# The last three modulation chunks of layer 0: one load step at a time in place of two

## The chip, the cores and the metric

The kernel runs on one core of one Trainium2 chip. The metric is device time in microseconds (us) of one execution; lower is better.

## The reference

The program is a two-layer trunk over 256 latent and 256 context tokens of width 2048. Layer 0 mixes tokens by centred pooling, layer 1 by neighbourhood attention; each is followed by a gated MLP of width 5504. Before every sub-layer, a normalised stream is scaled and shifted, and its result is gated, by vectors that are computed from a conditioning vector:

```python
silu_c, silu_cc = jax.nn.silu(c), jax.nn.silu(c_ctx)
for i in range(DEPTH):
    ml = (silu_c @ w_mod[i] + b_mod[i]).reshape(B, 6, 1, D)
    mc = (silu_cc @ w_mod[i] + b_mod[i]).reshape(6, 1, 1, D)
    a_lat = modulate(rms_norm(h, norm1_g[i]), ml[:, 0], ml[:, 1])
    ...
    h = h + ml[:, 2] * y_lat
    h = h + ml[:, 5] * conv_ffn(modulate(rms_norm(h, norm2_g[i]), ml[:, 3], ml[:, 4]), ...)
```

The change concerns `silu_c @ w_mod[0]` and `silu_cc @ w_mod[0]`, the modulation of layer 0: a matrix of 2048 x 12288 float32 (about 100 MB) is read once, for two vectors.

## The kernel before

**Chunks and steps.** The 12288 columns of layer 0's modulation are 24 chunks of 512. `mod_pe` works through one chunk in four steps. A step loads 2 tiles of 128 x 1024 float32 (512 KB each, line 131, tile `wm`), and multiplies them with the two vectors on TensorE in four products (line 207, tile `mod`), each in a 32-column strip of the array of its own (`tile_position`), so that the four run beside one another. The products of all four steps add up in one PSUM bank with the tag `m`, of which there is one. After the fourth step ScalarE copies the bank out (line 219, `modev`); at the start of the next chunk TensorE turns the copy by four transposes (line 224, `modt`), and VectorE sums and finishes it (line 226 and `finish_mod`).

**Pairs of steps.** In the kernel before, the first step of a pair (g = 0 or 2) only loads. The second one (g = 1 or 3) loads and then issues eight products in a row, its own four first, then those of the step held back. The first of the eight waits for all four loads of the pair; the others are tied behind it, so that nothing comes between them.

**Buffers.** `stage` hands out weight buffers in turn from the list `rooms`: six of its own and those lent from the activation tiles by `lend`. All weights pass through the same list. In the stretch that matters here the lent buffers have been taken back (`LENT`, at half 13 of group 3), so six buffers remain, three pairs: two 512 KB tiles for each step of modulation and two for each load of other weights. A load into a buffer waits, on the load queue (SP), until the buffer's last reader is done.

**What runs beside it.** `partial(g, ...)` computes the first eight blocks of layer 0's gate and up projections for input group g, with weights `wcg` (gate) and `wcu` (up), four blocks at a time; each load is split into a high part by a cast on ScalarE (line 147) and a low part by a subtraction on VectorE (line 149), and 48 matmuls follow (lines 566 to 568, `cg` and `cu`), beside a shift term (lines 549 and 582, `pwg`, `pwu`, `ptg`, `ptu`). Between them, at 32 places ("halves") for each g, `between` calls `need`, which pumps the generator of modulation steps to a count that grows by 20 in 32 halves. In group 3 the steps pumped are 79 to 96, of which 81 to 84 are chunk 20, 85 to 88 chunk 21, 89 to 92 chunk 22 and 93 to 96 chunk 23. Then the rest of layer 0's MLP follows, its first matmuls in line 653.

**Order.** The Python order gives priorities; the scheduler then sets each engine's instruction order at build time by its own estimate of when each instruction is ready. `tc.high_priority()` and `tc.issue_after(...)` adjust that. On the chip every queue runs in that order.

Of the kernel before, what the change touches and what calls it, by code (L numbers as in the profile page):

```python
# [59 lines left out]
def kernel(ctx: ExitStack, tc: tile.TileContext, xT, cxT, wmod, wg, wu, wd, wp,  # L60
# [10 lines left out]
    def bank(tag, name):  # L71

        if tag == "d" and nbank[0] is not None:
            nbank[0] += 1
            if nbank[0] % 4 == 0:
                tag = "m"
        return pp.tile([P, 512], F32, tag=tag, bufs={"gu": 4, "d": 3, "m": 1}[tag], name=name)
# [45 lines left out]
    fetched = []  # L123

    def load(src, cols, name):

        ts = []
        for j in range(0, cols, 1024):
            n = min(1024, cols - j)
            t = stage(f"{name}_{j}")  # L130
            fetched.append(nc.sync.dma_start(t[:, :n], src(j, j + n)).ins)
            ts.append((t, n))
        return ts
# [27 lines left out]
    def mod_tile(l, ch):  # L161

        return main.tile([P, 4, 2], F32, tag=f"modT{ch if ch < 20 else (l, ch)}", name=f"modT{l}_{ch}")

    def by_row(ps):

        return ps.rearrange("p (i j c) -> p i c j", i=4, j=4)[:, :, 0:2, :]
# [9 lines left out]
    def finish_mod(l, ch, streams, src):  # L177

        mt = src[0] if len(src) == 1 else mod_tile(l, ch)
        n = len(streams)  # L180
        which, q = divmod(ch, 4)

        def dup(name, a):
            return V(name)[:, a : a + 8].rearrange("p (i s) -> p i s", s=2)[:, :, 0:n]

        bias = dup(f"bm_{l}", 8 * ch)
        for b, v in enumerate(src):
            own = slice(32 * b, 32 * b + 32) if len(src) > 1 else slice(0, P)
            nc.vector.tensor_tensor(mt[own, :, 0:n], v, bias[own], op=ALU.add)
        if which in (1, 4):  # L190
            nc.vector.scalar_tensor_tensor(mt[:, :, 0:n], mt[:, :, 0:n], 1.0, dup(f"g{1 if which == 1 else 2}_{l}", 8 * q),
                                           op0=ALU.add, op1=ALU.mult)
        modT[l, ch] = mt

    def mod_pe(l, ch, sc, pool):

        ps = bank("m", f"mod{l}_{ch}")
        for g in range(4):
            ts = load(lambda a, b: wmod[l, ch, g, :, a:b], 2048, f"wm{l}_{ch}_{g}")
            if g % 2 == 0:  # L200
                held, first = ts, fetched[-2:]
            else:
                landing = first + fetched[-2:]
                with ExitStack() as behind:
                    for n, (gg, tt) in enumerate(((g, ts), (g - 1, held))):
                        for j in (2, 3, 0, 1):
                            ins = nc.tensor.matmul(ps[32 * j : 32 * j + 32, :], sc[:, 4 * gg + j, :],  # L207
                                                   tt[j // 2][0][:, 512 * (j % 2) : 512 * (j % 2) + 512],
                                                   start=(g == 1 and n == 0), stop=(g == 3 and n == 1),
                                                   tile_position=(0, 32 * j))  # L210
                            if n == 0 and j == 2:
                                for x in landing:
                                    tc.add_manual_dep(ins.ins, x.name, mybir.DependencyInfo(
                                        mybir.DependencyClass.Sync, mybir.DependencyReason.DATA), reason="whole")
                                behind.enter_context(tc.issue_after(ins.ins))
                                behind.enter_context(tc.high_priority())
            if g == 3:
                ev = pool.tile([P, 512], F32, tag="t2", name=f"modev{l}_{ch}")
                nc.scalar.copy(ev, ps)
            yield  # L220
        with tc.high_priority():
            p2 = bank("d", f"modt{l}_{ch}")
            for i in range(4):
                nc.tensor.transpose(p2[:, P * i : P * i + P], ev[:, P * i : P * i + P], ident)
        r = mod_tile(l, ch)
        nc.vector.tensor_reduce(out=r, in_=by_row(p2), axis=AX.X, op=ALU.add)
        finish_mod(l, ch, both, [r])
# [116 lines left out]
    with ExitStack() as ph0:  # L344
# [62 lines left out]
        with ExitStack() as phs:  # L407
# [32 lines left out]
            def mods():  # L440

                for g in range(4):
                    for w in (0, 1, 2, 4):
                        yield from mod_pe(0, 4 * w + g, sc, f0)
                    yield from mod_pe(0, 12 + g, sc, f0)
                    shifts(g)
                for q in range(4):
                    yield from mod_pe(0, 20 + q, sc, f0)
# [805 lines left out]
```

## Time and profile before

| | |
|---|---|
| median of 3 runs | 3062.89 us (3062.56 to 3066.64) |
| the profiled execution | 3060.9 us |
| its span, first to last instruction | 3059.1 us |
| mean granted TensorE clock | 0.989 |
| TensorE (PE) busy | 2977.4 us, 97% |
| VectorE (DVE) busy | 1939.4 us, 63% |
| ScalarE (ACT) busy | 1371.3 us, 45% |
| read from memory | 554.93 MB, 182 GB/s over the span |

Times in the profile are counted from the first instruction. PE is the matmul part of TensorE, PEld its weight loads, SPq the queue that issues the loads. In a row of the timeline, the first number is the start, the second the length, and `x16` a count of instructions (a product with float32 operands is two); a bracket tells how long the engine had been idle before it and what ended that. A granted clock of 1.00 is full speed.

### The profile page before, as it was taken

How to read it: one execution, taken by the hardware profiler on the slowest of the kernel's cores; microseconds unless marked ns; L12 is line 12 of the kernel's file. 1: busy time of each engine (PE TensorE's matmuls, PEld its weight loads, DVE VectorE, ACT ScalarE, POOL GpSimd, SP SyncE). 2: the span in 40 equal slices, each digit the busy share in tenths (PEclk: the TensorE clock that was granted, in tenths of full speed). 3: DMA queues.
4: the chain of work that ended last, by engine and by line, in shares of the span. 5: the costliest groups of instructions: out<-in, count | busy, mean ns of one | idle time of the engine just before them, and what ended most of it. 6: DMA issues, size and time to landing. Idle time of an engine off the chain costs nothing.

```text
span 3059.1 us, 40876 instructions
## 1 busy us (share of the span) xinstructions
PE 2977.4 (97%) x15082; PEld 2416.9 (79%) x15082; DVE 1939.4 (63%) x2748; ACT 1371.3 (45%) x2219; POOL 829.1 (27%) x823
## 2 busy tenths in 40 slices
PE   5999989999999999999999999999999999999998
PEld 2666668888888888888887888878888888888887
DVE  4455764386584857758586656474767666666666
ACT  3433455323333242433334444343545666666665
POOL 2111313303122030321312000000003566566665
PEclk9999989999999999999999999999999999999999
DMA  9888563384765747567482333333355555555563
GB/s 390 331 305 321 207 206 97 103 255 142 216 192 166 241 143 234 160 198 212 150 257 69 121 101 114 101 107 111 106 161 182 185 181 196 192 187 182 184 196 113
DMA packets 177927, 559.70 MB, mean 183 GB/s; under 512 B 17600, under 2 KB 22208, under 8 KB 177728
## 3 DMA queue, kind: packets, MB, share of 16 engines
q1 hardware_dynamic: 177728, 557.10, 55.7%
q8 instruction: 119, 1.95, 0.2%
q14 instruction: 80, 0.66, 0.1%
HBM read 554.93 MB, written 2.10 MB: 182 GB/s over the span
## 4 chain that ended last, share of the span: by engine, by line
PE 93%; DMA 2%; DVE 1%; POOL 1%; ACT 1%; issue 1%; SPq 0%; DVEq 0%; ACTq 0%; POOLq 0%
PE g L788 5%; PE u L788 5%; PE d L679 5%; PE d L680 5%; PE d L681 5%; PE d L835 4%; PE g L653 4%; PE g L655 4%; PE g L654 4%; PE u L655 4%; PE u L653 4%; PE u L654 4%; PE g L791 3%; PE u L791 3%; PE mod L207 2%; PE d L839 2%
## 5 line engine op out<-in xcount | busy, mean ns | idle before, releaser
L692 POOL TENSOR_TENSOR hl<-hl,dy 128x256 f32<-128x256 f32 x160 | 146.2, 914 | 941.8 <-ACT dy L691 941.6
L850 POOL TENSOR_TENSOR hl<-hl,dy 128x256 f32<-128x256 f32 x320 | 332.1, 1074 | 188.3 <-ACT dy L848 186.0
L262 DVE SCALAR_TENSOR_TENSOR macc<-wm,sc,macc 128x512 f32<-128x512 f32 (+1 forms) x360 | 328.8, 944 | 66.9 <-DMA wm<-wmod 66.2
L691 ACT ACTIVATE dy<-d,modT 128x256 f32<-128x256 f32 x320 | 133.1, 469 | 187.5 <-PE d L681 167.2
L692 POOL TENSOR_TENSOR hc<-hc,dy 128x256 f32<-128x256 f32 x160 | 129.4, 809 | 0.0
L848 ACT ACTIVATE dy<-d,modT 128x512 f32<-128x512 f32 x160 | 104.5, 684 | 43.0 <-PE d L839 41.5
L149 DVE TENSOR_TENSOR wd_2l<-wd,wd_2h 128x1024 fp32r<-128x1024 f32 (+1 forms) x44 | 54.5, 1245 | 107.8 <-ACT wd_2h L147 106.6
L207 PE MATMUL mod<-wm,sc 128*32 128x512 f32 x768 | 98.9, 641 | 15.2 <-DMA wm<-wmod 13.4
L937 POOL TENSOR_TENSOR rk<-rk,rp 128x256 f32<-128x256 f32 x16 | 13.2, 826 | 365.3 <-DVE rk L936 309.7
L149 DVE TENSOR_TENSOR wd_3l<-wd,wd_3h 128x1024 fp32r<-128x1024 f32 (+1 forms) x44 | 52.0, 1202 | 77.3 <-ACT wd_3h L147 75.9
L149 DVE TENSOR_TENSOR wd_1l<-wd,wd_1h 128x1024 fp32r<-128x1024 f32 (+1 forms) x44 | 53.7, 1224 | 54.4 <-ACT wd_1h L147 54.4
L487 POOL TENSOR_TENSOR pf<-ws,inv 128x256 f32<-128x256 f32 x32 | 29.3, 935 | 208.0 <-DVE ws L482 192.9
L149 DVE TENSOR_TENSOR wd_0l<-wd,wd_0h 128x1024 fp32r<-128x1024 f32 (+1 forms) x44 | 54.6, 1248 | 40.9 <-ACT wd_0h L147 40.9
L147 ACT CAST wd_1h<-wd 128x1024 fp32r<-128x1024 f32 (+1 forms) x44 | 45.3, 1032 | 74.8 <-PE u L654 49.4
L1026 ACT ACTIVATE sb<-sb,nm 128x512 f32<-128x512 f32 x64 | 46.1, 721 | 64.5 <-DVE nm L1022 63.3
L207 PEld LDWEIGHTS mod<-wm,sc 128*32 128x32 f32 x768 | 22.3, 114 | 65.5 <-issue 62.0
L147 ACT CAST wd_0h<-wd 128x1024 fp32r<-128x1024 f32 (+1 forms) x44 | 45.3, 1032 | 59.1 <-PE u L788 29.1
L814 DVE TENSOR_TENSOR actb<-sgb,actb 128x256 fp32r<-128x256 f32 x43 | 52.7, 1226 | 26.5 <-ACT actb L813 26.5
L679 PE MATMUL d<-act,wd_2h 128*128 128x512 f32 x172 | 67.1, 390 | 0.0
L681 PE MATMUL d<-act,wd_2l 128*128 128x512 f32 x172 | 66.9, 389 | 0.0
L680 PE MATMUL d<-act,wd_2h 128*128 128x512 f32 x172 | 66.9, 389 | 0.0
L679 PE MATMUL d<-act,wd_0h 128*128 128x512 f32 x172 | 66.9, 389 | 0.0
(1752 smaller groups left out, 9274.6 us busy)
## 6 DMA issues: line engine op xcount, KB each, us to landing
wm<-wmod SPq DMA_DIRECT2D x384, 512.0 KB, 6.1
wd<-wd SPq DMA_DIRECT2D x168, 512.0 KB, 4.4
wg<-wg SPq DMA_DIRECT2D x156, 512.0 KB, 4.7
wu<-wu SPq DMA_DIRECT2D x156, 512.0 KB, 4.5
wv<-wv SPq DMA_DIRECT2D x32, 512.0 KB, 3.7
wk<-wq SPq DMA_DIRECT2D x32, 512.0 KB, 4.0
wq<-wq SPq DMA_DIRECT2D x32, 512.0 KB, 3.6
wo<-wo SPq DMA_DIRECT2D x32, 512.0 KB, 4.2
```

Of the source, the lines that this page charges most:

```text
L149: eng.tensor_tensor(lo[:, :n], t[:, :n], hi[:, :n].bitcast(F32), op=ALU.subtract)
L262: nc.vector.scalar_tensor_tensor(acc[s], v, sc2[:, k, s : s + 1], acc[s], op0=ALU.mult, op1=ALU.add)
L653: nc.tensor.matmul(ps, hi[:, c : c + P], xh, start=(k == 0), stop=False)
L654: nc.tensor.matmul(ps, hi[:, c : c + P], xl, start=False, stop=False)
L655: nc.tensor.matmul(ps, lo[:, c : c + P], xh, start=False, stop=(k == KT - 1))
L679: nc.tensor.matmul(ps, hi[:, o : o + P], xh, start=(i == 0), stop=False)
L680: nc.tensor.matmul(ps, hi[:, o : o + P], xl, start=False, stop=False)
L681: nc.tensor.matmul(ps, lo[:, o : o + P], xh, start=False, stop=(i == n - 1))
L692: nc.gpsimd.tensor_tensor(h_of(s)[:, k, :], h_of(s)[:, k, :], y[:, s], op=ALU.add)
L788: nc.tensor.matmul(ps, hi[:, c : c + P], flat(B[k]), start=(k == 0), stop=False)
L791: nc.tensor.matmul(ps[:, T:], lo[:, c : c + P], B[k][:, 0], start=False, stop=(k == KT - 1))
L850: nc.gpsimd.tensor_tensor(hl[:, k, :], hl[:, k, :], y[:, q], op=ALU.add)
```

## The change

For chunks 21, 22 and 23 (`ch > 20`) every step now issues its own four products as soon as its own two loads have landed. The other 21 chunks keep their pairs and eight products in a row. The conditions that start and stop the sum in the bank are rewritten so that they hold for both.

```diff
         ps = bank("m", f"mod{l}_{ch}")
+        held = []
         for g in range(4):
             ts = load(lambda a, b: wmod[l, ch, g, :, a:b], 2048, f"wm{l}_{ch}_{g}")
-            if g % 2 == 0:
-                held, first = ts, fetched[-2:]
-            else:
-                landing = first + fetched[-2:]
+            held.append((g, ts, fetched[-2:]))
+            if ch > 20 or g % 2:
                 with ExitStack() as behind:
-                    for n, (gg, tt) in enumerate(((g, ts), (g - 1, held))):
+                    for n, (gg, tt, _) in enumerate(held[::-1]):
                         for j in (2, 3, 0, 1):
                             ins = nc.tensor.matmul(ps[32 * j : 32 * j + 32, :], sc[:, 4 * gg + j, :],
                                                    tt[j // 2][0][:, 512 * (j % 2) : 512 * (j % 2) + 512],
-                                                   start=(g == 1 and n == 0), stop=(g == 3 and n == 1),
-                                                   tile_position=(0, 32 * j))
+                                                   start=(g < 2 and (n == 0 and held[0][0] == 0)),
+                                                   stop=(g == 3 and gg == held[0][0]), tile_position=(0, 32 * j))
                             if n == 0 and j == 2:
-                                for x in landing:
+                                for x in sum((d for _, _, d in held), []):
                                     tc.add_manual_dep(ins.ins, x.name, mybir.DependencyInfo(
                                         mybir.DependencyClass.Sync, mybir.DependencyReason.DATA), reason="whole")
                                 behind.enter_context(tc.issue_after(ins.ins))
                                 behind.enter_context(tc.high_priority())
+                held = []
```

## The prediction

> **What bounds the kernel now.** I read the page first, then the chain of waits, then the windows around layer 0's last modulation chunks, then TensorE and the load queue instruction by instruction there.
>
> ```profile
> span 3059.1 us, 40876 instructions
> PE 2977.4 (97%) x15082; PEld 2416.9 (79%) x15082; DVE 1939.4 (63%) x2748; ACT 1371.3 (45%) x2219; POOL 829.1 (27%) x823
> PE 93%; DMA 2%; DVE 1%; POOL 1%; ACT 1%; issue 1%; SPq 0%; DVEq 0%; ACTq 0%; POOLq 0%
> L207 PE MATMUL mod<-wm,sc 128*32 128x512 f32 x768 | 98.9, 641 | 15.2 <-DMA wm<-wmod 13.4
> ```
>
> TensorE (PE) sets the end nearly everywhere; 2% of the chain is DMA. Of PE's idle time before the modulation products (line 207), 13.4 us waited for their weights. The changed chunks run in these stretches (columns: length, then PE, PEld, DVE, ACT, POOL busy, granted clock, DMA share, GB/s):
>
> ```profile
> 364.49:377.45 12.96, 12.96 (x88) 7.86 (x87) 9.13 (x17) 5.28 (x10) 3.72 (x3) 1.00 0.71 244
> 377.45:391.04 13.59, 13.59 (x68) 9.59 (x69) 12.82 (x25) 9.11 (x20) 2.92 (x2) 1.00 0.67 232
> 391.04:411.67 20.63, 10.96 (x58) 3.38 (x57) 9.40 (x20) 4.71 (x9) 1.45 (x1) 0.61 0.62 207
> 377.45:428.80 51.35, 40.07 (x213) 23.74 (x213) 34.12 (x62) 22.91 (x44) 7.79 (x5) 0.83 0.68 229
> ```
>
> Up to 391.04 PE is full. From there to 411.67 it is busy for 10.96 of 20.63 us, at a granted clock of 0.61, while the DMA engines are used for 0.62 of the time: nobody is at a limit, so this is a round trip between a buffer and its load. PE in that stretch:
>
> ```profile
> 375.82 0.60 PE L582 MATMUL ptu<-ident,peu 128*128 128x128 f32 x4
> 378.50 1.92 PE L207 MATMUL mod<-wm,sc 128*32 128x512 f32 x16
> 391.04 1.92 PE L207 MATMUL mod<-wm,sc 128*32 128x512 f32 x16
> 400.89 3.64 PE L207 MATMUL mod<-wm,sc 128*32 128x512 f32 x16 [7.93 <-DMA wm<-wmod]
> 405.31 1.12 PE L224 MATMUL modt<-ident,modev 128*128 128x128 f32 x4 [0.78 <-ACT modev L219]
> 408.24 3.64 PE L207 MATMUL mod<-wm,sc 128*32 128x512 f32 x16 [0.96 <-DMA wm<-wmod]
> 411.67 1.46 PE L549 MATMUL pwu<-wcu,sh 128*32 128x256 f32 x16
> 413.06 0.50 PE L566 MATMUL cu<-Ad,wcu_4h 128*128 128x512 f32 x1
> 424.17 1.92 PE L207 MATMUL mod<-wm,sc 128*32 128x512 f32 x16
> ```
>
> A row of 16 is one group of eight products (two instructions each). Counted back from the last, at 424.17, they are: 378.50 the second half of chunk 21, 391.04 and 400.89 the halves of chunk 22, 408.24 and 424.17 those of chunk 23. Two of them ran at half speed, 3.64 against 1.92 us. The loads' queue (start, length over all, count):
>
> ```profile
> 365.58 0.80 SPq L131 DMA_DIRECT2D wm<-wmod  x2
> 369.48 0.89 SPq L131 DMA_DIRECT2D wcg<-wg  x2
> 370.47 0.96 SPq L131 DMA_DIRECT2D wm<-wmod  x2
> 377.51 1.34 SPq L131 DMA_DIRECT2D wm<-wmod  x2
> 379.59 2.12 SPq L131 DMA_DIRECT2D wm<-wmod  x4
> 392.13 1.97 SPq L131 DMA_DIRECT2D wm<-wmod  x4
> 402.85 0.80 SPq L131 DMA_DIRECT2D wm<-wmod  x2
> 404.55 0.89 SPq L131 DMA_DIRECT2D wcu<-wu  x2
> 411.90 0.80 SPq L131 DMA_DIRECT2D wm<-wmod  x2
> ```
>
> Call the steps 85 to 96: 85-88 are the four of chunk 21, 89-92 of chunk 22, 93-96 of chunk 23. From step 87 on the code leaves six buffers, three pairs, taken in turn by 87, 88, the gate weights `wcg` (369.48), 89, 90, 91, 92, 93, the up weights `wcu` (404.55), 94, 95, 96. So 89 takes the pair of 87, 92 that of 89, `wcu` that of 91, 94 that of 92, 95 that of 93. Read that way, the queue says: step 87's load was issued at 365.58, but its products wait for step 88's (370.47), so its buffers come free in the group at 378.50. That group runs the newer step first, so 88's pair goes to step 90 (379.59) and 87's to step 89 (the later two of those four). Step 89 then sits in the group at 391.04, again as the older half, and step 92's load is the last pair at 392.13. PE waits 7.93 us for it.
>
> ```profile
> 393.51 7.25 DMA wm<-wmod
> 403.27 4.84 DMA wm<-wmod
> SPq L131 <- PE mod L207: 25.5, 9, 6.6
> wm<-wmod SPq DMA_DIRECT2D x2, 512.0 KB, 4.4
> wm<-wmod SPq DMA_DIRECT2D x2, 512.0 KB, 8.0
> ```
>
> The first two rows are from the chain of waits: issue to landing of the last load ahead of 400.89 and of 408.24. The third is the queue's own waits in 364 to 416 us: 25.5 us for modulation products to give buffers back. The last two are issue to landing of the pair at 365.58 (4.4 us, alone) and of step 89's pair (8.0 us, behind two others).
>
> **The change part by part.** No load, product, copy or transpose is added or dropped, and the order in which buffers are taken stays as it is. What changes is when a step may run and when it gives its buffers back.
>
> *Removed: holding the first step for the second.* Step 87 landed at about 365.58 + 0.4 + 4.4 = 370.4 (0.4 for the pair's second issue). Its place in the code is after 36 of the 48 up products that end at 375.82, so about 12 x 0.23 before that, at 373. Alone it gives its pair back at about 374 and not at 378.50 + 1.92 = 380.4. Step 89 then lands at about 374 + 0.4 + 4.4 = 378.8 and not at about 380.6 + 8.0 = 388.6. Its place is after 6 of the 48 gate products, about 380, so step 92 gets its buffers at about 381 in place of 393; behind two other pairs, for which 8.0 us is the row, it lands by 389, when PE is still in the gate products. Step 91 stands after 24 gate products and three groups, 377.45 + 5.5 + 3.7 = 386.7, so `wcu` is issued at about 388 and not at 404.55, and is in by 394. PE needs for the second stretch its 13.59 us, one step more than now (91 and 92 come in, 87 has left) and a set of transposes, and arrives at `wcu` at about 394 too. So these go: 7.93 + 0.96 us of waits for loads, 0.78 for the copy of a chunk's sums, which then has products beside it, and the half clock, 2 x (3.64 - 1.92) = 3.44. Sum 13.1 us. What hides the loads from here on is the gate and up products; without that cover each step would show its 4.4 to 8.0 us.
>
> *Added: more groups.* Chunks 21 to 23 make six groups of eight into twelve of four, six more.
>
> ```profile
> 400.89 2.00 PE mod L207 x8
> 364.17 0.39 PE L568 MATMUL cu<-Ad,wcu_0l 128*128 128x512 f32 x1
> 364.49 1.92 PE L207 MATMUL mod<-wm,sc 128*32 128x512 f32 x16
> 366.34 0.50 PE L566 MATMUL cu<-Ad,wcu_0h 128*128 128x512 f32 x1
> 366.68 0.40 PE L567 MATMUL cu<-Ad,wcu_0h 128*128 128x512 f32 x1
> 366.92 0.40 PE L568 MATMUL cu<-Ad,wcu_0l 128*128 128x512 f32 x1
> ```
>
> The first row is the chain's: the first four of the group at 400.89 took 2.00 us, all eight 3.64. So four cost 1.64 more, and entering a group 0.36, at half clock. At full clock the steps into and out of a group are 0.32 and 0.34 us where two ordinary products lie 0.24 apart (366.68 to 366.92), 0.18 us together. I take 0.3 (nearer the row that holds the whole cost): 6 x 0.3 = 1.8 us, between 1.1 and 2.2.
>
> *Moved: the gate weights behind step 88.* Now both steps 85 and 86 end in one group, newer first, so `wcg` (in 86's pair) goes at 369.48 ahead of step 88 at 370.47. Alone, 85 ends first, and step 88's pair goes ahead. The row below is an earlier stretch, by the modulation products alone (length, PE, PEld, ACT busy, clock, DMA share, GB/s).
>
> ```profile
> 36.00:300.00 264.00, 65.14 (x528) 15.06 (x528) 9.27 (x16) 0.97 0.89 333
> ```
>
> At its rate, 333 GB/s at a share of 0.89, a pair of 1 MB takes 2.8 us, so `wcg` comes up to that much later, with the cast and subtraction behind it and the gate products behind those. Step 87's group, now ahead of it, fills about 1.2 us of that. I take 1.2 us, between 0 and 2.8.
>
> *Left over: the up weights' cast.* After `wcu` lands come a cast on ACT and its lower half on DVE. Now they lie between 411.5 and 413.06 with the products of line 549 beside them. I take 1.0 us of wait, from 0 (step 93's group covers it) to 2.3 (a cast and a subtraction shown bare).
>
> ```profile
> L147 ACT CAST wcu_4h<-wcu x2: 1044/1045/1046, 411.5 to 412.5; 128x1024 fp32r<-128x1024 f32 x2
> L149 DVE TENSOR_TENSOR wcu_4l<-wcu,wcu_4h x2: 1218/1222/1227, 412.6 to 413.8; 128x1024 fp32r<-128x1024 f32 x2
> ```
>
> *Waits added.* The first product of every step now carries the wait for its own two loads. Behind it in PE's queue stand the gate and up products; if a step stands too early, they wait. A chunk's first product also needs the one sum bank copied out one step earlier than now; the copy (line 219) is 0.6 us and ACT is busy 22.91 of 51.35 us, so I cost it at nothing, 0.78 us (the row at 405.31) if it shows.
>
> Sum: 13.1 - 1.8 - 1.2 - 1.0 = 9.1 us gained. Three limits check it. PE has 51.35 - 40.07 = 11.3 us idle there plus 3.4 of half clock: 14.7. The DMA engines held a share of 0.89 over 264 us (the stretch from 36 us), so 0.68 x 51.35 / 0.89 = 39.2 us, 12.1 to gain. DVE needs 34.12 us; it would bind beyond 17. After 428.80 PE is the limit again, and the gain should reach the end whole.
>
> The profiled execution took 3060.9 us, 1.8 above its span and 2.0 below the median of the three timed runs, 3062.89. So 3060.9 - 9.1 = 3051.8, and as a median 3053.8. With every cost at its end the gain is 13.1 - 1.1 = 12.0 or 13.1 - 2.2 - 2.8 - 2.3 = 5.8: 3050.9 to 3057.1. The walk above, taken at its word, would give more than the sum, since PE would then hardly idle at all; its times are best cases that follow one another, so I keep the sum and let PE's limit set the low end of the range.
>
> **Clock.** The row is 400.89: after 7.93 us without work, the same group took 3.64 in place of 1.92 us, in a stretch with a granted clock of 0.61. The Trainium skill, "TensorE: Matmul & The Clock Gate", section "HAM oscillation — how this bites in real kernels", says that bursts of some 2 us, each followed by a wait for a load of 3 to 5 us, start cold every time, and that the remedy is to put bursts together. That speaks against the change, which halves the bursts; this trace agrees that one long wait halves the clock. The third rival is such a course, worked out from rows.
>
> **The rivals.**
>
> *No change.* The queue of PE is fixed when the program is built. If steps 89 and 90 both stay behind the gate products, where their pair stands now (391.04), 89's buffers come free only half a group sooner, 0.96 us; over the two round trips that is 1.9, against 1.8 for the groups. Time 3062.9. For it: the group at 391.04 really did run after all gate products. Against: its load was due at about 388.6, and it is step 87's holding that made it so late.
>
> *Up weights behind one more step (slower).* The queue already departs from the code's order: step 94's load (402.85) stands ahead of `wcu` (404.55). If it also puts step 95 ahead of `wcu`, then `wcu` waits for step 93's group, as 95 does at 411.90. Nothing can cover this, since all up products need `wcu`: 411.90 + 0.80 - 404.55 = 8.2 us, plus 1.8, so about 3072.9. The change turns to a loss once the cast of `wcu` starts less than 1.8 us ahead of its present 411.5. Against: 91's pair, which `wcu` takes, is given back two steps ahead of 93's.
>
> *Every step cold (slower).* If each of the eight steps from 89 on is met by a wait long enough to halve the clock, each costs 3.64/2 - 1.92/2 = 0.86 us more, 6.9 in all; 3.4 of it is paid already. With the 1.8 and the old waits kept, 3062.9 + 5.3 = 3068.2. Against: there are 48 gate and 48 up products to stand between them.
>
> **How the numbers follow.** The forecast has 0.68, no change 0.16, up weights 0.11, every step cold 0.05. About 0.2%, 6.1 us, is what a measurement of this kernel can tell from no change; the likeliest case's lower gain is close to that. So faster 0.68, same 0.16, slower 0.16. The range runs from PE's limit less the cheapest groups, 14.7 - 1.1 = 13.6, so 3049.3, to just past no change, 3063.5; it leaves out the slower cases.
>
> **What would show it.** Right: step 89's load at about 374, step 92's near 381 and `wcu` near 388; no wait over 3 us before line 207 after 377; groups of 8 instructions of about 1 us; the granted clock near 1.00 between 391 and 411; the first product of line 653, now at 428.80, near 420. Wrong: `wcu` issued after 404, rows of four at 2.00 us, or a new wait of cg products for `wcg` of over 3 us. If the stage ends earlier and the span does not, the loss is after 428.80.

## The result and the profile after

| | before | changed |
|---|---|---|
| median of 10 runs | 3064.14 us (3062.56 to 3066.77) | 3055.34 us (3051.73 to 3061.99) |
| ratio | | 0.9972, 95% interval 0.9963 to 0.9981 |
| profiled execution | 3060.9 us, span 3059.1 | 3053.4 us, span 3051.6 |

The change saves 8.8 us by the medians, clear of the interval. The first lines of the changed kernel's page show that hardly anything else moved:

```profile
span 3051.6 us, 40877 instructions
PE 2974.9 (97%) x15082; PEld 2414.5 (79%) x15082; DVE 1932.7 (63%) x2748; ACT 1372.5 (45%) x2219; POOL 827.9 (27%) x823
```

The same matmuls run; PE is busy 2.5 us less (it was busy at half clock before) and the span is 7.5 us shorter. The windows of the stretch (columns as in the prediction) show where. From 391 to 402 PE is busy for 9.20 of 11 us at a granted clock of 1.00, where before it had 0.61 and was idle half of the time, and the DMA engines work at a share of 1.00 in the stretch ahead of it, 0.67 before.

```profile
377.40:391.00 13.60, 12.54 (x80) 7.22 (x78) 9.97 (x18) 8.58 (x17) 3.44 (x3) 1.00 1.00 347
391.00:402.00 11.00, 9.20 (x49) 5.45 (x46) 9.39 (x18) 7.13 (x14) 2.09 (x2) 1.00 0.81 255
402.00:413.00 11.00, 11.00 (x75) 6.54 (x74) 9.60 (x21) 6.94 (x15) 2.06 (x1) 1.00 0.75 265
```

PE's timeline in the changed kernel (the product is now line 206; `x8` is a group of four products):

```profile
370.84 1.92 PE L206 MATMUL mod<-wm,sc 128*32 128x512 f32 x16
375.64 1.07 PE L206 MATMUL mod<-wm,sc 128*32 128x512 f32 x8
379.59 1.06 PE L206 MATMUL mod<-wm,sc 128*32 128x512 f32 x8
384.45 1.06 PE L206 MATMUL mod<-wm,sc 128*32 128x512 f32 x8 [1.06 <-DMA wm<-wmod]
389.96 1.06 PE L206 MATMUL mod<-wm,sc 128*32 128x512 f32 x8
393.00 1.06 PE L206 MATMUL mod<-wm,sc 128*32 128x512 f32 x8
397.30 0.39 PE L568 MATMUL cg<-Ad,wcg_4l 128*128 128x512 f32 x1
397.62 1.07 PE L206 MATMUL mod<-wm,sc 128*32 128x512 f32 x8
398.62 0.50 PE L568 MATMUL cg<-Ad,wcg_4l 128*128 128x512 f32 x1
398.95 0.39 PE L566 MATMUL cg<-Ad,wcg_4h 128*128 128x512 f32 x1
401.61 0.50 PE L566 MATMUL cu<-Ad,wcu_4h 128*128 128x512 f32 x1 [1.80 <-ACT wcu_4h L147]
423.00 0.50 PE L653 MATMUL g<-A,wg_8h 128*128 128x512 f32 x1 [2.11 <-DVE late L376]
```

Steps 85 and 86 run back to back (370.84); 87 to 92 are the six single groups that follow. The wait of 7.93 us is gone, no group runs at half clock, and two smaller waits stand in its place: 1.80 us for the cast of the up weights and 2.11 us ahead of line 653. The load queue of the changed kernel:

```profile
372.79 0.95 SPq L131 DMA_DIRECT2D wcg<-wg  x2
376.74 0.81 SPq L131 DMA_DIRECT2D wm<-wmod  x2
385.53 0.81 SPq L131 DMA_DIRECT2D wm<-wmod  x2
394.09 0.90 SPq L131 DMA_DIRECT2D wcu<-wu  x2
```

These are the gate weights, step 89, step 92 and the up weights. Before, they stood at 369.48, 380.6, 393 and 404.55.

Absolute times of two profiled executions must be lined up first. The part ahead of the stage is the same code, yet it ends at a different time in every execution; the first matmul of line 320 marks its end:

```profile
344.46 1.02 PE L320 MATMUL n2b<-n2d,ones 128*128 128x512 f32 x2
```

```profile
346.90 1.02 PE L320 MATMUL n2b<-n2d,ones 128*128 128x512 f32 x2
```

The first row is the kernel before, the second the changed one, 2.44 us later. So I measure the stage from line 320 to the first matmul of line 653: 428.80 - 344.46 = 84.3 us before, 423.00 - 346.90 = 76.1 after. That is 8.2 us saved, against 7.5 in the whole span.

One thing more differs between executions behind that mark. In the kernels of the table below, PE waits there 3.4 us for `sh` ahead of line 549, and the clock after this wait is not the same everywhere. The first row is the kernel before, the second the one with the older step first (see below):

```profile
352.07 1.96 PE L549 MATMUL pwg<-wcg,sh 128*32 128x256 f32 x16 [3.42 <-DVE sh L438]
```

```profile
353.34 1.09 PE L549 MATMUL pwg<-wcg,sh 128*32 128x256 f32 x16 [3.42 <-DVE sh L438]
```

Where the products behind this wait ran at half clock for some us, the first group of modulation products behind line 320 starts 20.0 to 20.1 us after it; elsewhere it starts after 18.9. Nothing ahead of that group was edited, so these 1.1 us do not belong to the edits, and different kernels are better compared from that group on (364.49 before, 366.94 in the changed kernel): 64.3 us to line 653 before, 56.1 after, again 8.2 saved.

### The profile page after: what moved, and what is told of

It is laid out like the page before. It is cut to its first block, busy times and chain, and to the rows that moved or that the text cites. A ratio compares the mean times of both kernels' runs of the same rounds, so it can differ in the third digit from the quotient of the medians.

```text
span 3051.6 us, 40877 instructions
## 1 busy us (share of the span) xinstructions
PE 2974.9 (97%) x15082; PEld 2414.5 (79%) x15082; DVE 1932.7 (63%) x2748; ACT 1372.5 (45%) x2219; POOL 827.9 (27%) x823
## 4 chain that ended last, share of the span: by engine, by line
PE 91%; DVE 3%; DMA 3%; POOL 1%; issue 1%; ACT 1%; SPq 0%; DVEq 0%; POOLq 0%; ACTq 0%
PE g L788 5%; PE u L788 5%; PE d L679 5%; PE d L680 5%; PE d L681 5%; PE d L835 4%; PE g L653 4%; PE g L655 4%; PE g L654 4%; PE u L655 4%; PE u L653 4%; PE u L654 4%; PE g L791 3%; PE u L791 3%; PE d L839 2%; PE mod L206 2%
## 5 line engine op out<-in xcount | busy, mean ns | idle before, releaser
L147 ACT CAST wd_1h<-wd 128x1024 fp32r<-128x1024 f32 (+1 forms) x44 | 45.3, 1032 | 81.2 <-PE u L654 55.1
L1026 ACT ACTIVATE sb<-sb,nm 128x512 f32<-128x512 f32 x64 | 46.1, 721 | 64.3 <-DVE nm L1022 63.2
L679 PE MATMUL d<-act,wd_0h 128*128 128x512 f32 x172 | 66.9, 389 | 0.0
L680 PE MATMUL d<-act,wd_0h 128*128 128x512 f32 x172 | 66.9, 389 | 0.0
```

The source lines that it names most:

```text
L679: nc.tensor.matmul(ps, hi[:, o : o + P], xh, start=(i == 0), stop=False)
L680: nc.tensor.matmul(ps, hi[:, o : o + P], xl, start=False, stop=False)
```

## The experiments

The stage times, each from one profiled execution. The kernel of all chunks is left out, since line 320 stands elsewhere in its order. The last column but one counts from the first modulation group behind line 320.

| kernel | ratio of times, 95% interval | stage, us | from the first group, us | longest wait of PE for a modulation load, us |
|---|---|---|---|---|
| before | 1 | 84.3 | 64.3 | 7.9 |
| changed (chunks 21 to 23 single) | 0.9972 (0.9963 to 0.9981) | 76.1 | 56.1 | 1.1 |
| chunk 21 single | 0.9974 (0.9965 to 0.9984) | 77.8 | 58.9 | 2.8 |
| chunks 22 and 23 single | 0.9980 (0.9971 to 0.9989) | 77.5 | 58.6 | 3.8 |
| steps 91 and 92 single | 0.9994 (0.9985 to 1.0003) | 81.2 | 62.3 | 7.6 |
| pairs, older step first | 0.9978 (0.9969 to 0.9988) | 76.5 | 57.6 | 1.5 |
| pairs, fourth pair of buffers | 0.9963 (0.9949 to 0.9976) | 74.5 | 54.4 | 0.8 |
| pairs, ten buffers to half 17, eight to half 21 | 0.9954 (0.9942 to 0.9967) | 71.4 | 51.2 | none |
| changed, fourth pair | 0.9972 (0.9961 to 0.9983) | 73.4 | 54.4 | none |
| pairs, older step first, fourth pair | 0.9981 (0.9973 to 0.9990) | 77.9 | 57.8 | none |
| changed, weights of block 8 loaded early | 0.9972 (0.9962 to 0.9982) | 77.0 | 56.9 | 0.7 |
| changed, `late` written ahead | 0.9969 (0.9958 to 0.9981) | 75.1 | 56.2 | 1.3 |
| changed, both of these | 0.9972 (0.9963 to 0.9982) | 77.1 | 58.2 | 1.2 |

### Which chunks

Three edits of the one condition:

```diff
-            if ch > 20 or g % 2:
+            if ch == 21 or g % 2:                  # chunk 21
+            if ch > 21 or g % 2:                   # chunks 22 and 23
+            if (ch, g) == (22, 2) or g % 2:        # steps 91 and 92
```

> Only chunk 21 goes one step at a time. Theory A (the prediction's): the delay is one chain that begins with step 87, whose buffers are held for step 88; freeing them alone lets step 89 load at about 377 in place of 380 and land at about 384 in place of 388.6, so most of the gain is here: 5 us or more, about 3059. Theory B: what costs is step 91 held for step 92, because the up weights take step 91's buffers and all up products wait for them; this kernel leaves that as it was, so 92 is still met late. At most 2 us gained, 3062 to 3064, up weights issued after 400. Theory C (clock): the waits stay about as they are and only PE's half clock matters; no change either.

> Chunks 22 and 23 go one step at a time, 21 in pairs. Theory A: step 89 still loads at 380 to 381 and lands at 388, so at most half of the gain is left, 4 us or less, 3060 or more. Theory B: step 91 no longer waits for 92, the up weights are issued at about 392 in place of 404.55 and the first up product is near 400; the whole gain of 8 to 9 us stays, about 3055, and perhaps 0.6 us more since there are two groups fewer.

> One pair alone is parted: steps 91 and 92 of chunk 22 each issue their own four products; all other steps stay in pairs. Theory A: no more than 2 us gained. Theory B: step 91 (landed about 384) runs right behind the group of 89 and 90 at about 393, the up weights are issued at about 394 and land at about 399 in place of 411.5; 7 us or more gained, 3054 to 3057, with one more group in place of six. Theory C (the half clock is the gain): depends on whether a wait over 3 us remains ahead of step 92.

Chunk 21 alone kept 8.8 us by the medians (3054.93 against 3063.74), as theory A expects; by the traces, from the first group on, it kept 5.4 of the 8.2 us. Theory A's forecast for the second kernel failed, though: without chunk 21, chunks 22 and 23 still gave 7.0 us (3056.76), and not 4 or less. Steps 91 and 92 alone gave 2.7 us, with an interval that reaches past 1. So theory B is wrong as well. The timelines of the three tell why, in this order:

```profile
387.00 1.92 PE L206 MATMUL mod<-wm,sc 128*32 128x512 f32 x16
396.91 1.92 PE L206 MATMUL mod<-wm,sc 128*32 128x512 f32 x16 [2.77 <-DMA wm<-wmod]
403.36 3.64 PE L206 MATMUL mod<-wm,sc 128*32 128x512 f32 x16 [2.70 <-DMA wm<-wmod]
```

```profile
391.96 2.78 PE L206 MATMUL mod<-wm,sc 128*32 128x512 f32 x24
398.58 1.30 PE L206 MATMUL mod<-wm,sc 128*32 128x512 f32 x8 [3.85 <-DMA wm<-wmod]
```

```profile
393.23 2.78 PE L206 MATMUL mod<-wm,sc 128*32 128x512 f32 x24
403.58 1.94 PE L206 MATMUL mod<-wm,sc 128*32 128x512 f32 x8 [7.56 <-DMA wm<-wmod]
```

With chunk 21 single, the pair of steps 89 and 90 runs at 387.00, 21.8 us behind the first modulation group and not 26.6 as before, so step 92 is met after 2.77 us. With chunk 21 in pairs, steps 89 to 91 run in one go at 392 or 393 (`x24`) and 92 follows; it is met after 3.85 us in one kernel and 7.56 us in the other.

Up to step 92, PE's order is the same in these two kernels but for one thing: the first runs step 89 ahead of 90, the other 90 ahead of 89. Step 92 takes the buffers of 89. Its last load, from issue to landing, in the first kernel and then in the second:

```profile
393.48 4.97 DMA wm<-wmod
```

```profile
395.71 7.73 DMA wm<-wmod
```

Counted from the start of the `x24` group, the load went out 1.0 us sooner in the first kernel, and it landed 2.8 us faster, since in the second the pair of step 93 (394.33) was issued ahead of it. Together that is the 3.7 us between the two waits, with nothing else moved ahead of them in PE's queue. So the time at which a buffer is given back, and the order of the loads that follows from it, set this wait.

With only steps 91 and 92 single, the up weights were issued at 396.36, 10 us earlier than before when lined up by the first group, but the group of step 92 stands ahead of the up products in PE's queue. PE waited for step 92 first, then ran it and the transposes and shift products behind it at half clock, and the up products began at 410.07, only 5 us earlier. That is what theory B left out: an early load gives nothing back while another wait stands before its reader. Nor does theory C hold: chunk 21 alone kept the whole gain by the times, and two thirds of it by the traces, with one group still at half clock (403.36), and its waits were shorter. The earlier release helps at either end of the chain from step 87 to the up weights; the two ends do not add.

### All chunks

```diff
-            if ch > 20 or g % 2:
+            if True:
```

> All 24 chunks go one step at a time: 42 groups more than the changed kernel. With 0.3 us for a group on a full PE, up to 12.6 us slower than the changed kernel, about 3067; where PE waits for loads anyway (the first 50 us) the groups are free. If freeing buffers early helped everywhere, it would instead be faster than 3055. The row for a group of four against one of eight gives the cost of a group in the middle of the gate and up products.

Measured 3055.91 us, ratio 0.9980 (0.9971 to 0.9989): neither 3067 nor a further gain. The cost of 42 more groups does not show in the time. In the trace there are only some 30 more, since several steps run back to back (76 rows of modulation products against 47). In the stretch from 36 to 300 us the DMA share is 0.88 at 330 GB/s in this kernel and 0.89 at 332 GB/s in the changed one; PE is busy for 249.05 and for 247.84 of the 264 us. The loads may set the pace there, and for 300 us, not the 50 that I had allowed, but PE is not far from full either. No run took one of the two limits away, so where the cost went stays open.

### More buffers, pairs kept

```diff
-LENT = {(2, 31): range(4, 12), (3, 6): range(8, 12), (3, 13): ()}
+LENT = {(2, 31): range(4, 12), (3, 6): range(8, 12), (3, 13): range(10, 12), (3, 21): ()}   # fourth pair
+LENT = {(2, 31): range(4, 12), (3, 6): range(8, 12), (3, 17): range(10, 12), (3, 21): ()}   # ten, then eight
```

> The kernel before, pairs and eight products in a row kept, but two of the lent buffers stay in the list from half 13 to half 21, so steps 87 to 92 take four pairs of buffers in turn and not three. Buffer theory: step 92's load need not wait for the group at 391, is issued 8 us earlier or more, and the wait of 7.9 us shrinks below 3; 4 to 8 us faster, 3056 to 3060, without any product moved. If it is the number of products in a row that matters, or the order in which a pair runs, nothing changes (3062 to 3065).

> The kernel before with all ten buffers kept until half 17 and eight until half 21; pairs as before. If the count of buffers is still short after the fourth pair, up to 3 us better than the room kernel (3049.5); if the loads then only land earlier than needed, no better than it (3052 to 3053.5); it turns worse if the normalised tiles that go into the lent buffers come late, seen as PE waits before line 653 or behind it.

Both are the kernel before with pairs and eight products in a row. The first measured 3052.43 us against 3063.69, a gain of 11.3 us where 4 to 8 were expected; the second measured 3048.82 against 3062.78. Their intervals overlap, so whether the second is better than the first is not shown. The second reaches step 92's group without a wait for its load, and then the up products after 0.21 us:

```profile
392.05 1.92 PE L207 MATMUL mod<-wm,sc 128*32 128x512 f32 x16
396.48 0.50 PE L566 MATMUL cu<-Ad,wcu_4h 128*128 128x512 f32 x1 [0.21 <-ACT wcu_4h L147]
```

So the gain needs no fewer products in a row; more buffers alone bring it. It is not true, though, that no product moved. The code of the products is the same, but the scheduler, which goes by its own estimates, gave the groups earlier places in PE's queue. The group of steps 87 and 88 stood behind four of the 48 gate products before and stands ahead of all of them in both kernels; that of 89 and 90 stood behind all 48, and stands behind 25 in the first and 15 in the second. How much of the gain is the earlier loads and how much the earlier places, these two kernels do not tell. The normalised tiles that go into the lent buffers did not come late: PE's wait before line 653 stayed at 0.9 us, as before, and behind it the profile lists no wait of PE up to 560 us.

### The order within a pair

```diff
-                    for n, (gg, tt) in enumerate(((g, ts), (g - 1, held))):
+                    for n, (gg, tt) in enumerate(((g, ts), (g - 1, held))[:: -1 if ch > 20 else 1]):
```

> The kernel before; for chunks 21 to 23 a pair still waits for all four loads and runs eight products in a row, but the older step's four come first, so the older step's buffers are given back first. Buffer theory: step 89's buffers come free half a group earlier and step 92's load goes ahead of step 93's (at 392.1 in place of 393.0 and first in the queue), lands near 397.5 in place of 400.8, and the wait of 7.9 us falls to about 5; 2 to 4 us faster, 3060 to 3062. If only the number of buffers held counts, no change (3063 to 3065).

Measured 3056.07 us against 3062.78, 0.9978 (0.9969 to 0.9988): 6.7 us, more than the 2 to 4 expected, for a change of order that adds no group.

```profile
387.82 1.92 PE L207 MATMUL mod<-wm,sc 128*32 128x512 f32 x16
394.64 1.92 PE L207 MATMUL mod<-wm,sc 128*32 128x512 f32 x16 [1.46 <-DMA wm<-wmod]
401.88 1.58 PE L549 MATMUL pwu<-wcu,sh 128*32 128x256 f32 x16 [3.49 <-DMA wcu<-wu]
```

The expected 5 us of wait are 1.46, and the clock is kept (1.92 us, no 3.64). I had counted a single round trip, about 3 us: step 92's load ahead of step 93's, as in the two rows at 393.48 and 395.71 above. In the trace the whole chain moved. The loads now land in the order in which they are used, and the scheduler put the group of steps 89 and 90 behind 34 of the gate products in place of 48. That group runs at 387.82 and not at 391.04, 3.4 us earlier when lined up by the first modulation group (23.2 us behind it against 26.6). A new wait of 3.49 us for the up weights takes part of that back.

### Adding the cures up

The first kernel is the changed one with the fourth pair of buffers, the second has pairs, the older step first and the fourth pair.

> The changed kernel with the fourth pair of buffers of the room kernel (lent until half 21). If early release and more buffers cure one and the same wait, the two don't add: 3051 to 3055, no better than the room kernel (0.9963) by more than 1 us, and the six additional groups cost about 2 us of PE time in it. If they cure different waits, up to 8 us more: 3045 to 3048.

> The older step first in chunks 21 to 23, and the fourth pair of buffers until half 21. In the room kernel PE still idles under 1 us at each of four places in this stretch, so little is left for the order to gain: 3051 to 3053.5, same as the room kernel within 1.5 us.

They measured 3053.65 us, 0.9972 (0.9961 to 0.9983), and 3057.40 us, 0.9981 (0.9973 to 0.9990), no better than the fourth pair alone (0.9963). The second came out slower than the 3051 to 3053.5 us expected. In the first the up weights were issued at 388.12, the earliest of the kernels with a fourth pair only, and yet nothing came of it at the end. PE's waits, first kernel and then second:

```profile
PE g L653 <- DVE late L376: 3.7, 1, 3.7
```

```profile
PE g L653 <- DVE late L376: 5.5, 1, 5.5
```

What is gained earlier is given back ahead of line 653, where 0.9 us were waited before and 2.1 in the changed kernel. The two cures work on one wait, and behind it stands the next one. It need not stand there: the kernel with ten buffers reaches its first up product just as early as the first of these two (30.9 us behind the first modulation group against 32.1) and waits 0.9 us ahead of line 653.

### The wait ahead of line 653

Three kernels on top of the changed one: the weights of block 8 loaded before three buffers are taken from the list; VectorE's first two multiplications of `late` (here `held_times_norm`) written ahead of the finish of chunk 23; both.

```diff
+        early = [load(lambda a, b: wsrc[0, NS][:, a:b], 2048, f"w{nm}0_{NS}") for nm, wsrc in (("g", wg), ("u", wu))]
         ring = range(NW // 2 + 1, NW + 1)
...
+            made = [held_times_norm(NC, q) for q in range(2)]
             need(97)
...
-        r6 = late(NC)
+        r6 = late(NC, made)
```

> The changed kernel, and the gate and up weights of block 8 are loaded while all six buffers are still in the list, before three of them are taken away for layer 1's modulation. In the changed kernel PE's end of the stage (419.4 to 423.0) follows the up weights' load at 412.95, its cast and the subtractions on DVE. If that load sets the end: it is issued near 407 to 412 without waiting for the gate weights' split, and line 653 starts 1 to 2 us earlier; 3053 to 3054. If it is the copy of chunk 23's sums and the work behind it on DVE, no change (3055).

> The changed kernel, and VectorE's two multiplications that empty the first two held banks of block 6 are written ahead of the finish of chunk 23 in place of behind it. Line 653's first product waits for one of these banks. If VectorE's order sets the end of the stage: line 653 starts 1 to 2.5 us earlier, 3053 to 3054.5. If the weights do, no change (3055).

> Both edits of the two kernels before this one on top of the changed kernel. If each removes a cause of its own, the gains add, up to 3.5 us (3051.5); if they are two ends of one wait, it is no better than the better one.

They measured 3055.74, 3054.23 and 3054.38 us, 0.9972 (0.9962 to 0.9982), 0.9969 (0.9958 to 0.9981) and 0.9972 (0.9963 to 0.9982): no change against the changed kernel. The late load of the weights is not the cause, since the wait stayed at 2.3 us with the early load. The second edit does not test its theory: the scheduler left the multiplications where they were, behind the reduction of chunk 23, as VectorE's timeline of that kernel shows.

```profile
416.58 2.01 DVE L149 TENSOR_TENSOR wg_8l<-wg,wg_8h 128x1024 fp32r<-128x1024 f32 x1 [0.21 <-ACT wg_8h L147]
418.51 0.18 DVE L226 TENSOR_REDUCE modT<-modt 128x8 f32<-128x32 f32 x1
418.73 0.17 DVE L189 TENSOR_TENSOR modT<-modT,vt 128x8 f32<-128x8 f32 x1
418.81 0.18 DVE L595 TENSOR_REDUCE puu<-ptu 128x8 f32<-128x32 f32 x1
418.91 0.68 DVE L369 TENSOR_TENSOR late<-cg,n2acc 128x512 f32<-128x512 f32 x1
```

The first row shows what stands directly ahead of the reduction: a subtraction of block 8's weights (line 149). One stands there in the kernel with the early load (419.10, 1.23 us) and in the changed kernel (420.72, 1.23 us) too; in the kernel before, VectorE had been idle for 2.76 us when the reduction came. So in these kernels the splitting of the weights holds up the reduction, also where they were loaded early. No run moved it, and whether these 2 us can be had by order alone stays open.

## Why the prediction was right, point by point

**The total.** Forecast 9.1 us, measured 8.8 by the medians and 8.2 in the stage. The mechanism, buffers held by the first step of a pair, is borne out by three kernels that leave the change out and keep their pairs: two with more buffers and one with another order gained 6.7 to 14.0 us. In these three the scheduler also moved groups in PE's queue, so the earlier release alone is not measured there. Where PE's order stayed the same (the rows at 393.48 and 395.71), releasing the older step first took 3.7 us off the wait. The forecast's chain through step 87 is one way in, as chunk 21 alone shows, but not the only one: the prediction did not see that chunks 22 and 23 without 21 would give most of it too.

**Waits and clock, 13.1 us.** Of the 7.93 + 0.96 us of load waits 1.06 remain (384.45, step 89); the copy's 0.78 us and the 3.44 us of half clock are gone. So 12.0 us went. The prediction counted on none staying. It gave step 89's load 4.4 us, the time of a pair that flies alone, and a landing at about 378.8. In the changed kernel the last load of that step took 7.14 us, with two other pairs issued ahead of it (371.93 and 372.79), and the DMA share is 1.00 from 377.40 to 391.00:

```profile
377.17 7.14 DMA wm<-wmod
```

It landed at 384.31, which is 381.9 when lined up.

**Groups, 1.8 us at 0.3 each.** From 397.30 to 398.95 a group of four takes 1.65 us, less two ordinary steps of 0.23 that is 1.19; the group of eight at 364.49 took 2.05 by the same count. So entering costs 2 x 1.19 - 2.05 = 0.33 us, 2.0 for six. The half-clock row (0.36) was the better of the two bounds. Steps 85 and 86 ran back to back, so only five groups came on top. Even so, the products of lines 206 or 207 and 566 to 568, added up from start to start behind the first modulation group and without waits, took 46.1 us before, 42.7 without the 3.44 of half clock, and 44.9 after: 2.2 us for the groups, the upper end of the term.

**Gate weights, 1.2 us.** They did go behind step 88, at 372.79: 0.9 us later when lined up. PE did not wait for them, since steps 87 and 88 both run ahead of the gate products now. The cost was 0, the lower bound. The prediction had let only step 87 cover it.

**The up weights' cast, 1.0 us.** Measured 1.80, within the bounds (0 to 2.3).

**Not foreseen: line 653.** The wait there grew from 0.88 to 2.11 us, behind VectorE's order. It was written that PE is the limit again after 428.80 and that the gain reaches the end whole; 1.2 us of it were lost at that door. With the measured terms, 12.0 - 2.2 - 1.8 - 1.2 = 6.8. Transposes and shift products now run at full clock where they had run at half: from 405.31 to 406.22 one set of transposes took 0.91 us, at full clock the chain of waits has 0.44, twice, and the 16 instructions of line 549 took 1.39 and now take 1.02, 1.3 us in all. The wait for the copy of chunk 23's sums fell from 0.73 to 0.43 us. That makes 8.4 against the 8.2 measured. The forecast's total was closer than its terms, and that closeness is luck: it had the gate weights too dear and the cast and line 653 too cheap, and missed the half clock of the small products.

**Signposts.** Lined up by line 320 (2.4 us), step 89's load stands at 374.3 (said: 374), step 92's at 383.1 (381), the up weights at 391.7 (388), the first matmul of line 653 at 420.6 (420). No wait for a load is over 3 us, and the clock is 1.00 from 391 to 413.

**The rivals.** *No change* and *up weights behind one more step* did not occur. *Every step cold* did not occur either: all single groups of the changed kernel took 1.06 or 1.07 us. Other products stand between them, and no wait for a load was over 1.06 us. The Trainium skill, "TensorE: Matmul & The Clock Gate", section "HAM oscillation — how this bites in real kernels", warns of this course for short bursts with waits of 3 to 5 us for a load between them. In two other kernels, where waits stayed longer, the half clock came back: 1.94 us for a group of four after 7.56 us (steps 91 and 92 alone), 3.64 for eight after 2.70 us.

**What the edits leave.** The fastest kernel by the medians is not the changed one: the kernel before with its lent buffers kept longer measured 3048.82 us, 14.0 under the kernel before, with no group added.

## What to carry to other kernels

Where an engine idles for a load while the DMA engines are not full, look for the reader that holds the buffer which that load needs, and follow the buffers in turn: which load takes whose place, and what released it. A group that waits for several loads holds the first of them for as long as the last one takes; more buffers, an earlier release or just the older half first all helped here, and they did not add up. Check first whether a buffer that is idle can be lent a little longer, as that costs no instruction.

## What the runs showed that was not expected

The order within a group of eight moves each release by about 1 us, and yet the older step first gained 6.7 us. The rows at 393.48 and 395.71 tell a part of it: the load that is needed first also goes ahead of another pair in the queue, which was worth 2.8 us more at a single step. The scheduler also gave the groups earlier places in PE's queue, and the share of that is not known. Forty-two more groups of four in the code did not show in the total. And the half clock set in after a PE wait of 2.70 us (3.64 us for eight products at 403.36, chunk 21 alone) but not after one of 2.77 us in the same kernel (1.92 us at 396.91); in the first case waits and transposes filled the 4.5 us before it, in the second dense matmuls ran up to the wait. Nor does the length of a wait settle it: after the same 3.42 us ahead of line 549, the same 16 instructions took 1.96 us in one kernel and 1.09 in another. What decides these runs do not show.
